# Residual rows moved to VectorE in a two-layer decoder trunk, with two smaller moves in the tail and the gate

## The chip, the cores and the metric

The kernel runs on one core of one Trainium2 chip. The metric is the device time of one execution in microseconds (us), the median of several runs. A run with a profile also gives its span, from the first to the last instruction, and for every instruction its engine, start and duration. The engines are named as in the profile: PE (TensorE, with PEld for its weight loads), DVE (VectorE), ACT (ScalarE), POOL (GpSimd) and SP (SyncE, here only a queue for DMAs).

## What is computed

Four sublayers follow one another on x of 512 rows (tokens) by 1024 columns: 0 is a hybrid mixer (sparse attention and a spatial gate), 1 and 3 are SwiGLU feed-forward layers (FFN) with 2816 hidden units, 2 is a gated short convolution (the "odd" layer). Each is wrapped in the same way:

```python
def residual_update(x, c, ada_w, ada_b, ln_g, ln_b, sublayer):
    shift, scale, gate = ada_modulation(c, ada_w, ada_b)     # silu(c) @ w + b, three rows of 1024
    out = sublayer(x * (1 + scale) + shift)
    return layer_norm(ALPHA * x + (1 + gate) * out, ln_g, ln_b)
```

All is float32; ALPHA is the square root of 2.

## The kernel before

**Tiles.** Rows are cut into four row tiles of 128 (`ST`), kept in one SBUF tensor `xr` of 128 x 4 x 1024. Weights come in units of 128 x 2048, loaded in two halves into `raw` (four buffers, SP's queue, L443). Every float32 operand of a matmul is split into a rounded high part and a remainder, so each product takes three matmuls: for a weight unit ACT makes `hi` (L472) and DVE makes `lo` (L476); weights of an output projection are first multiplied by the gate row, `raw` by `gateb` on DVE (L462). The class `Stream` does this some units ahead of PE, in the order in which they will be used.

**Stages.** An input tile (`in_tile`, matmuls on L524) is 24 matmuls of 128 x 512 into one of four PSUM buffers; ACT or DVE take it out, and `split` makes the high part (L1880, ACT) and the remainder (L1881, DVE) of the activation. An output chunk (`out_chunk`, matmuls on L536) adds eight output tiles of 128 x 512 into `xr` by DVE (`out_evac`, L541). The order on each engine's queue is the order in which the Python code issues the instructions; only sublayer 0 and the begin of sublayer 1 follow an order written out by hand.

**From one sublayer to the next.** `tail_norm` runs the last output chunk row tile by row tile. Per row tile: evacuation, statistics (`stats`, L569, L574), a Newton iteration for the inverse square root (`newton`, L635 to L646, nine instructions on 128 x 1), the normalisation of `xr` in place (`norm`, L611, DVE), PE transposes (L658), the affine of the next sublayer's modulation (ACT, L668), high part (ACT, L675) and remainder (`low`, L678, DVE) of the transposed tile `h`. While row tile 2 is handled, ACT has begun a weight unit of the next sublayer; its two remainders (L476) are issued when row tile 3 is. `start_in` then begins four input tiles on the first half of the rows (256 columns), so that the transposes of row tile 3, hooked in after the second of them, have time; the second halves follow.

**The residual.** After the normalisation `xr` holds the plain normalised value; what the next output chunks add to is ALPHA times LayerNorm's result. `Norm.rows` loads the rows of ln_g and ln_b to all partitions (POOL's DMA queue, L559, L560), and POOL scales them by -ALPHA and ALPHA (L562, L564); `Norm.residual` multiplies and adds them to `xr`, two POOL instructions of 128 x 1024 for each row tile (L628, L629). All four row tiles are issued right behind `start_in`, before the second halves.

**The modulation's gate.** `ada_steps` is a generator that is advanced by `background()`, once after each tile: it loads 512 KB of ada_w at a time into `ar` (two buffers, ACT's queue, L344), adds eight products to `acc` on DVE (L330, L332), and sums over partitions by a matmul against ones (L364), from which DVE makes half of the row `gateb` (L365). The last of these, the gate of sublayer 3, is appended at the start of the odd layer.

Of the kernel before, what the change touches and what calls it, by code (L numbers as in the profile page):

```python
# [11 lines left out]
ALU = mybir.AluOpType  # L12
# [6 lines left out]
ST = S // P  # L19
KT = D // P  # L20
HID = 2816
ALPHA = 4.0 ** 0.25
# [200 lines left out]
def trunk(ctx: ExitStack, tc: tile.TileContext, x, c, ada_w, ada_b, ln_g, ln_b, even_w_in,  # L223
# [320 lines left out]
    class Norm:  # L544
# [9 lines left out]
        def rows(self):  # L554
            s = self.s
            l, w = divmod(s, 2)
            self.rowg = fpool[0].tile([P, D], F32, name="rowg", tag="rowg", bufs=1)
            self.rowb = fpool[0].tile([P, D], F32, name="rowb", tag="rowb", bufs=1)
            pool.dma_start(self.rowg, ln_g[l, w:w + 1, :].to_broadcast([P, D]))  # L559
            pool.dma_start(self.rowb, ln_b[l, w:w + 1, :].to_broadcast([P, D]))  # L560
            a = 1.0 if s == 3 else ALPHA
            pool.tensor_scalar(self.rowg, self.rowg, -a, None, op0=ALU.mult)  # L562
            if s != 3:
                pool.tensor_scalar(self.rowb, self.rowb, a, None, op0=ALU.mult)  # L564

        def stats(self, t, half, c=slice(0, 512)):
            if half == 0:
# [7 lines left out]
            return mv  # L575

        def rstd(self, t):
            return self.newton(self.aggr(t), pool if self.s < 3 else dve if t == 3 else nc.scalar)

        def store(self, t, mv, y):  # L580

# [41 lines left out]
                f()  # L623
            self.lows = []

        def residual(self, t):
            z = xr[:, t, :]
            pool.tensor_tensor(z, z, self.rowg, op=ALU.mult)  # L628
            pool.tensor_tensor(z, z, self.rowb, op=ALU.add)  # L629

    def newton(e, var, v, hv, y, q):

# [1171 lines left out]
    def tail_norm(acts, us, norm):  # L1804

        ws.get(us[-1], 0)
        pend, conv = None, ()
        for t in range(ST):
            pp = [out_tile(half) for half in range(2)]
            if t == 0:  # L1810
                for half in range(2):
                    out_mms(pp[half], acts, us, t, half, range(3), True, False)
            for half in range(2):
                if t == 0:
                    out_mms(pp[half], acts, us, t, half, [3], False, True)
                    out_evac(pp[half], t, half)
                    norm.stats(t, half)
                else:
                    n = 256 if (norm.s, t, half) == (3, 3, 1) else 512
                    for a in range(0, 512, n):  # L1820
                        c = slice(a, a + n)
                        if a:
                            pp[half] = ps.tile([P, 512], F32, name="po", tag="tr")
                        out_mms(pp[half], acts, us, t, half, range(4), True, True, c)
                        out_evac(pp[half], t, half, c)
                        norm.stats(t, half, c)
                if norm.s < 3 and half == 0 and t:
                    norm.norm(t - 1, *pend)
                    norm.low()
            pend = norm.rstd(t)  # L1830
            if norm.s == 3:
                norm.store(t, *pend)
            if t == 2 and ws.ready < min(us[-1] + 3, len(ws.units)):
                conv = ws.pieces()
                for i in range(2):
                    if conv[0]:
                        conv[0](i, dve)
                    conv[1](i)
            if t == 3 and conv:
                for i in range(2):  # L1840
                    conv[2](i, dve)
            if t and norm.s != 3:
                norm.transpose(t - 1)
        if norm.s == 3:
            return
        norm.norm(3, *pend)
        norm.low()

    def start_in(units, norm):
# [29 lines left out]
    def split(f, a, k):  # L1879
        act(a[0][:, k, :], f, AF.Copy)  # L1880
        dve.tensor_tensor(a[1][:, k, :], f, a[0][:, k, :], op=ALU.subtract)  # L1881
# [12 lines left out]
    def run_ffn(s, prev, cfg):  # L1894
        sizes, starts, ins, outs = cfg
        norm = Norm(s)
        acts = {}
        for ci in range(6):
            acts[ci] = new_act()
            for pr in range(sizes[ci] // 2):  # L1900
                m = starts[ci] + 2 * pr
                ug, uu = ins[m]
                if m == 0:
                    tl = prev.tiles or start_in([(ug, 0), (ug, 1), (uu, 0), (uu, 1)], prev)
                    if s == 1:
                        prev.rows()
                    for t in range(ST):
                        prev.residual(t)
                if ci == 3 and pr == 0:
                    norm.rows()  # L1910
                sg = []
                for q in range(4):
                    u = (ug, uu)[q // 2]
                    if m == 0:
                        p = tl[q]
                        in_tile(p, u, q % 2, prev.h, prev.second, 2 if q < 2 else 1)
                    else:
                        p = pm.tile([P, S], F32, name="pi", tag="mm")
                        in_tile(p, u, q % 2, prev.h, ahead=3)
                    if q < 2:  # L1920
                        f = fp.tile([P, S], F32, name="sg", tag="sg", bufs=3)
                        act(f, p, AF.Silu)  # L1922
                        sg.append(f)
                    else:
                        f = sg[q - 2]
                        dve.tensor_tensor(f, f, p, op=ALU.mult)  # L1926
                        split(f, acts[ci], 2 * pr + q - 2)
                    background()
                if pr == 0 and ci > 0:
                    out_chunk(acts.pop(ci - 1), outs[ci - 1], sizes[ci - 1])  # L1930
                    if s == 1 and ci == 1:
                        bg.extend([ada_steps(2, (0, 1, 2, 3)), ada_steps(2, (4, 5)),
                                   ada_steps(3, (0, 1, 2, 3))])
        if s == 1:
            drain_background()
            mod_finish(2)
            mod_finish(3)
        tail_norm(acts_of(acts[5]), outs[5], norm)
        tail_hooks(norm)
        return norm  # L1940

    def run_odd(s, prev):
        norm = Norm(s)
        acts = {}
        bg.append(ada_steps(3, (4, 5)))
        for pr in range(4):
            uc, uz, ub = o_in[pr]
            if pr == 2:
                norm.rows()
            if pr % 2 == 0:  # L1950
                acts[pr // 2] = new_act()
            if pr == 0:
                tl = start_in([(uc, 0), (uc, 1), (uz, 0), (uz, 1)], prev)
                for t in range(ST):
                    prev.residual(t)
            cz = []
            for q in range(6):
                u = (uc, uz, ub)[q // 2]
                j = 2 * pr + q % 2
                if pr == 0 and q < 4:  # L1960
                    p = tl[q]
                    in_tile(p, u, q % 2, prev.h, prev.second, 2 if q < 2 else 1)
                else:
                    p = pm.tile([P, S], F32, name="pi", tag="mm")
                    in_tile(p, u, q % 2, prev.h, ahead=3)
                if q < 2:
                    f = fp.tile([P, S + 2], F32, name="cz", tag="cz", bufs=2)
                    pool.memset(f[:, 0:2], 0.0)
                    act(f[:, 2:], p, AF.Copy)
                    cz.append(f)  # L1970
                elif q < 4:
                    f = cz[q - 2]
                    dve.tensor_tensor(f[:, 2:], f[:, 2:], p, op=ALU.mult)
                    y = fp.tile([P, S], F32, name="y", tag="sg", bufs=3)
                    dve.tensor_scalar(y, f[:, 2:], pc[:, j, 10:11], None, op0=ALU.mult)
                    dve.scalar_tensor_tensor(y, f[:, 1:S + 1], pc[:, j, 9:10], y,
                                             op0=ALU.mult, op1=ALU.add)
                    dve.scalar_tensor_tensor(y, f[:, 0:S], pc[:, j, 8:9], y,
                                             op0=ALU.mult, op1=ALU.add)
                    cz[q - 2] = y  # L1980
                else:
                    f = cz[q - 4]
                    dve.tensor_tensor(f, f, p, op=ALU.mult)
                    split(f, acts[pr // 2], j % 4)
                background()
                if pr == 2 and q == 3:
                    out_chunk(acts[0], o_out[0], 4)
        drain_background()
        tail_norm(acts_of(acts[1]), o_out[1], norm)
        tail_hooks(norm)  # L1990
        return norm
# [33 lines left out]
```

## Time and profile before

| what | value |
|---|---|
| median of 3 runs | 1273.43 us (1273.17 to 1279.45) |
| the profiled execution | 1270.58 us |
| its span | 1268.9 us |
| mean granted TensorE clock in it | 0.986 |
| busy share PE, DVE, ACT, POOL | 95%, 63%, 35%, 18% |

In the rows of a timeline the first number is the start in us from the span's begin, the second the duration, then engine, line, operation and out<-in; `x4` merges four instructions, and a bracket gives the idle time of the engine before it and what ended that. A row of a table of waits reads: who waited, for whom, us in total, times, longest. A row of stretches gives for each of PE, PEld, DVE, ACT and POOL the busy us and the number of instructions, then the granted clock of PE (1.00 is full), the busy share of the DMA engines and GB/s. A row of one line gives the shortest, the median and the longest duration in ns, then the first and last start.

### The profile page before, as it was taken

Reading aid. Unit: us, or ns where it says so; the run is one execution under the profiler, and the core shown is the slowest. Engines: PE = TensorE matmul, PEld = TensorE weight load, DVE = VectorE, ACT = ScalarE, POOL = GpSimd, SP = SyncE. Lnnn points to the kernel's source line nnn. Section 1 sums busy time; section 2 is a strip of 40 time slices with the busy share of each in tenths; the row PEclk is TensorE's granted clock in tenths of the full one; section 3 lists DMA queues with packets and bytes.
Section 4 is the critical chain, followed back from the end, with each engine's and each line's share of the span. In section 5 each row is a group of like instructions: output and inputs, shape, how many; then the busy total and the mean of one; then the engine's idle time right before and its main releaser. Section 6 shows DMA issues by size and latency. Waiting matters only on the chain.

```text
span 1268.9 us, 15462 instructions
## 1 busy us (share of the span) xinstructions
PE 1205.6 (95%) x5939; PEld 987.7 (78%) x5939; DVE 797.1 (63%) x1264; ACT 446.3 (35%) x776; POOL 231.4 (18%) x283
## 2 busy tenths in 40 slices
PE   5999999899989999999998799999899999999996
PEld 4777767678878888888887688887888888888885
DVE  5776567886766665657567875466874353535446
ACT  2472257985232122213125232124332121313224
POOL 3230013485810000000005420002800000000005
PEclk9899999999999999999999899999999999999998
DMA  9794651241366554547431463240253232323301
GB/s 298 209 282 129 210 181 50 62 139 43 105 195 195 169 167 162 172 147 222 144 100 50 144 222 100 67 131 3 100 166 100 67 128 72 108 92 100 100 1 67
DMA packets 121466, 164.74 MB, mean 130 GB/s; under 512 B 5861, under 2 KB 87085, under 8 KB 121392
## 3 DMA queue, kind: packets, MB, share of 16 engines
q1 hardware_dynamic: 105552, 132.33, 33.4%
q10 hardware_dynamic: 14208, 26.75, 6.4%
q0 software_dynamic: 1632, 4.67, 1.2%
q8 instruction: 46, 0.75, 0.2%
q14 instruction: 28, 0.23, 0.1%
HBM read 161.63 MB, written 2.10 MB: 129 GB/s over the span
## 4 chain that ended last, share of the span: by engine, by line
PE 82%; DVE 9%; DMA 3%; issue 2%; ACT 2%; POOL 2%; SPq 0%; DVEq 0%; ACTq 0%
PE pi L524 45%; PE po L536 23%; PE pi L1267 5%; DVE h L678 2%; DVE lo L476 1%; PE ph L1456 1%; PE po L1106 1%; PE ptp L1623 1%; DMA ar<-in_ada_w_dram 1%; DVE xr L611 1%; PE pi L859 1%; DVE xr L541 1%; DVE bst L569 1%; PE pc L1023 1%; PE pvo L1638 1%
## 5 line engine op out<-in xcount | busy, mean ns | idle before, releaser
L524 PE MATMUL pi<-h,hi 128*128 128x512 f32 (+1 forms) x2016 | 580.1, 373 | 2.2 <-DVE h L678 2.2
L524 PEld LDWEIGHTS pi<-h,hi 128*128 128x128 f32 x2016 | 367.8, 190 | 70.0 <-DVE h L678 2.6
L524 PE MATMUL pi<-h,lo 128*128 128x512 f32 (+1 forms) x1008 | 373.9, 371 | 0.0
L472 ACT ACTIVATE hi<-raw 128x1024 fp32r<-128x1024 f32 (+1 forms) x186 | 187.4, 1045 | 285.9 <-PE po L536 105.9
L476 DVE TENSOR_TENSOR lo<-raw,hi 128x1024 fp32r<-128x1024 f32 (+1 forms) x178 | 223.9, 1296 | 94.6 <-ACT hi L472 92.9
L524 PEld LDWEIGHTS pi<-h,lo 128*128 128x128 f32 x1008 | 190.8, 189 | 33.3
L541 DVE TENSOR_TENSOR xr<-xr,po 128x512 f32<-128x512 f32 x129 | 87.5, 681 | 130.2 <-PE po L536 130.0
L536 PE MATMUL po<-hi,ah 128*128 128x512 f32 (+1 forms) x420 | 165.9, 395 | 3.5 <-DVE xr L541 3.3
L536 PE MATMUL po<-hi,al 128*128 128x512 f32 (+1 forms) x420 | 165.1, 393 | 0.0
L536 PE MATMUL po<-lo,ah 128*128 128x512 f32 (+1 forms) x420 | 165.0, 393 | 0.0
L536 PEld LDWEIGHTS po<-hi,ah 128*128 128x128 f32 x420 | 79.4, 189 | 22.8 <-DVE xr L541 5.3
L536 PEld LDWEIGHTS po<-hi,al 128*128 128x128 f32 x420 | 79.4, 189 | 18.0
L536 PEld LDWEIGHTS po<-lo,ah 128*128 128x128 f32 x420 | 79.4, 189 | 17.7
L1880 ACT ACTIVATE ah<-sg 128x512 fp32r<-128x512 f32 x44 | 27.8, 632 | 173.6 <-DVE sg L1926 173.6
L1926 DVE TENSOR_TENSOR sg<-sg,pi 128x512 f32<-128x512 f32 x44 | 30.2, 687 | 90.4 <-PE pi L524 83.7
L635 POOL TENSOR_SCALAR v<-mv 128x1 f32<-128x1 f32 x12 | 4.7, 394 | 406.6 <-DVE mv L574 406.4
L462 DVE TENSOR_TENSOR raw<-raw,gateb 128x1024 f32<-128x1024 f32 x60 | 75.3, 1292 | 4.3 <-DMA raw<-in_even_w_out_dram 4.2
L332 DVE SCALAR_TENSOR_TENSOR acc<-ar,cs,acc 128x512 f32<-128x512 f32 x84 | 64.9, 773 | 7.3 <-DMA ar<-in_ada_w_dram 5.5
L1922 ACT ACTIVATE sg<-pi 128x512 f32<-128x512 f32 x44 | 26.3, 598 | 120.9 <-PE pi L524 120.8
L588 POOL TENSOR_TENSOR xr<-xr,rowg 128x512 f32<-128x512 f32 x6 | 8.2, 1359 | 325.7 <-ACT xr L587 325.7
L1267 PE MATMUL pi<-hi,h 128*128 128x512 f32 (+1 forms) x192 | 59.8, 377 | 0.0
L1881 DVE TENSOR_TENSOR al<-sg,ah 128x512 fp32r<-128x512 f32 x44 | 33.1, 752 | 30.8 <-ACT ah L1880 30.8
(256 smaller groups left out, 1363.0 us busy)
## 6 DMA issues: line engine op xcount, KB each, us to landing
raw<-in_ffn_w_in_dram SPq DMA_DIRECT2D x88, 512.0 KB, 4.5
ar<-in_ada_w_dram ACTq DMA_DIRECT2D x48, 512.0 KB, 4.3
raw<-in_ffn_w_out_dram SPq DMA_DIRECT2D x44, 512.0 KB, 4.1
ar<-in_ada_w_dram SPq DMA_DIRECT2D x24, 512.0 KB, 5.3
raw<-in_odd_w_in_dram SPq DMA_DIRECT2D x24, 512.0 KB, 4.5
raw<-in_even_w_in_dram SPq DMA_DIRECT2D x10, 512.0 KB, 5.3
aw<-in_ada_w_dram SPq DMA_DIRECT2D x8, 512.0 KB, 6.3
aw<-in_ada_w_dram SPq DMA_DIRECT2D x4, 1024.0 KB, 8.9
```

The lines of the kernel that those rows point to most:

```text
L332: dve.scalar_tensor_tensor(acc, r, cs[:, k:k + 1], acc, op0=ALU.mult, op1=ALU.add)
L462: e.tensor_tensor(z[:, k, :], z[:, k, :], gateb[fold == 2], op=ALU.mult)
L472: act(hl[0][:, i * n0:i * n0 + n0], raw(i), AF.Copy)
L476: e.tensor_tensor(hl[1][:, sl], self.raw.pop(2 * u + i), hl[0][:, sl], op=ALU.subtract)
L524: mm(p[:, sl], w, h[z][k // 4][:, k % 4, sl], start=k == 0 and i == 0, stop=k == KT - 1 and i == 2)
L536: mm(p[:, c], s_, w[:, k % 2, c0], start=first and i == 0, stop=last and i == n - 1)
L541: dve.tensor_tensor(z, z, p[:, c], op=ALU.add)
L1267: mm(tiles[t], s_, w[:, q, :], start=k == 0 and z == 0, stop=k == 7 and z == 2)
L1880: act(a[0][:, k, :], f, AF.Copy)
L1881: dve.tensor_tensor(a[1][:, k, :], f, a[0][:, k, :], op=ALU.subtract)
L1922: act(f, p, AF.Silu)
L1926: dve.tensor_tensor(f, f, p, op=ALU.mult)
```

## The change

The residual is done by DVE with two `scalar_tensor_tensor` instructions to a row tile, which take ALPHA as their scalar, so that POOL no longer scales the rows (only sublayer 3's ln_g is still negated). They are issued one by one: in an FFN behind the tiles of the first two chunks, in the odd layer behind the last two tiles of the first pair and the six of the second. The Newton iteration of row tile 3 goes from POOL to DVE in sublayers 1 and 2 too. The normalisation of row tile 3 and the transposes of row tile 2 are issued ahead of the two weight remainders. The gate of sublayer 3 is appended at the odd layer's second pair, behind the six tiles of the first.

```diff
@@ Norm.rows
-            a = 1.0 if s == 3 else ALPHA
-            pool.tensor_scalar(self.rowg, self.rowg, -a, None, op0=ALU.mult)
-            if s != 3:
-                pool.tensor_scalar(self.rowb, self.rowb, a, None, op0=ALU.mult)
+            if s == 3:
+                pool.tensor_scalar(self.rowg, self.rowg, -1.0, None, op0=ALU.mult)
@@ Norm.rstd
-            return self.newton(self.aggr(t), pool if self.s < 3 else dve if t == 3 else nc.scalar)
+            return self.newton(self.aggr(t), dve if t == 3 else pool if self.s < 3 else nc.scalar)
@@ Norm.residual
-        def residual(self, t):
-            z = xr[:, t, :]
-            pool.tensor_tensor(z, z, self.rowg, op=ALU.mult)
-            pool.tensor_tensor(z, z, self.rowb, op=ALU.add)
+        def residual(self):
+
+            for t in range(ST):
+                z = xr[:, t, :]
+                dve.scalar_tensor_tensor(z, z, -ALPHA, self.rowg, op0=ALU.mult, op1=ALU.mult)
+                yield
+                dve.scalar_tensor_tensor(z, self.rowb, ALPHA, z, op0=ALU.mult, op1=ALU.add)
+                yield
@@ tail_norm
+            if t == 3 and norm.s != 3:
+                norm.norm(3, *pend)
+            if t and norm.s != 3:
+                norm.transpose(t - 1)
             if t == 3 and conv:
                 for i in range(2):
                     conv[2](i, dve)
-            if t and norm.s != 3:
-                norm.transpose(t - 1)
-        if norm.s == 3:
-            return
-        norm.norm(3, *pend)
         norm.low()
@@ run_ffn
-                    for t in range(ST):
-                        prev.residual(t)
+                    res = prev.residual()
...
+                    if ci < 2 and pr == 0:
+                        for _ in range((0, 1, 1, 1, 2, 1, 1, 1)[4 * ci + q]):
+                            next(res)
                     background()
@@ run_odd
-        bg.append(ada_steps(3, (4, 5)))
...
-                for t in range(ST):
-                    prev.residual(t)
+                res = prev.residual()
+            if pr == 1:
+                bg.append(ada_steps(3, (4, 5)))
...
+                if 4 <= 6 * pr + q < 12:
+                    next(res)
                 background()
```

## The prediction

> **What bounds the kernel now.** I read the page first, then the PE engine's own table of waits, then the timeline of each engine around those waits.
>
> ```profile
> span 1268.9 us, 15462 instructions
> ...
> PE 1205.6 (95%) x5939; PEld 987.7 (78%) x5939; DVE 797.1 (63%) x1264; ACT 446.3 (35%) x776; POOL 231.4 (18%) x283
> ```
>
> PE is the bound: only 63 us of the span are without a matmul. An edit that gives PE no less work can win only from these gaps and from the speed at which PE restarts after them. So the question is which gaps belong to the lines of the diff. The PE rows of the table of waits (total, times, longest):
>
> ```profile
> PE pt L658 <- DVE xr L611: 9.2, 4, 3.9
> ...
> PE pa L364 <- DVE acc L332: 8.2, 1, 8.2
> ...
> PE po L536 <- DVE xr L541: 4.0, 3, 3.3
> PE pi L524 <- DVE h L678: 2.2, 2, 1.1
> ```
>
> These four hang on the code around the change. In the PE timeline they stand at three places: the first FFN, the entry to the odd layer and the entry to the second FFN.
>
> ```profile
> 357.87 0.50 PE L536 MATMUL po<-hi,ah 128*128 128x512 f32 x1 [3.29 <-DVE xr L541]
> ...
> 688.98 0.28 PE L524 MATMUL pi<-h,lo 128*128 128x256 f32 x1
> 693.19 0.61 PE L658 MATMUL pt<-ident,xr 128*128 128x128 f32 x2 [3.93 <-DVE xr L611]
> ...
> 704.28 0.38 PE L524 MATMUL pi<-h,hi 128*128 128x256 f32 x1 [1.11 <-DVE h L678]
> ...
> 722.65 2.08 PE L364 MATMUL pa<-acc,ones 128*128 128x512 f32 x2 [8.21 <-DVE acc L332]
> ...
> 894.59 1.90 PE L658 MATMUL pt<-ident,xr 128*128 128x128 f32 x8 [3.93 <-DVE xr L611]
> ...
> 905.67 0.39 PE L524 MATMUL pi<-h,hi 128*128 128x256 f32 x1 [1.11 <-DVE h L678]
> ```
>
> Together 3.29 + 3.93 + 1.11 + 8.21 + 3.93 + 1.11 = 21.6 us. All end on DVE. Why DVE is late shows in five DVE rows, two POOL rows, and the minimum/median/maximum of two DVE lines over the whole run:
>
> ```profile
> 684.92 0.21 DVE L574 BATCH_NORM_AGGREGATE mv<-bst 128x2 f32<-128x12 f32 x1
> 685.05 2.31 DVE L476 TENSOR_TENSOR lo<-raw,hi 128x1024 fp32r<-128x1024 f32 x2
> 690.23 2.81 DVE L611 TENSOR_SCALAR xr<-xr,mv,y 128x1024 f32<-128x1024 f32 x1 [2.88 <-POOL y L646]
> 692.96 11.26 DVE L678 TENSOR_TENSOR h<-v,h 128x512 fp32r<-128x512 f32 x4
> ...
> 721.06 1.54 DVE L332 SCALAR_TENSOR_TENSOR acc<-ar,cs,acc 128x512 f32<-128x512 f32 x2 [4.02 <-DMA ar<-in_ada_w_dram]
> ```
>
> ```profile
> 690.15 2.34 POOL L628 TENSOR_TENSOR xr<-xr,rowg 128x1024 f32<-128x1024 f32 x1
> ...
> 709.07 2.74 POOL L629 TENSOR_TENSOR xr<-xr,rowb 128x1024 f32<-128x1024 f32 x1
> ```
>
> ```profile
> L611 DVE TENSOR_SCALAR xr<-xr,mv,y x12: 796/813/2812, 280.4 to 891.6; 128x1024 f32<-128x1024 f32 x12
> ```
>
> ```profile
> L678 DVE TENSOR_TENSOR h<-v,h x22: 673/693/2900, 297.1 to 902.7; 128x512 fp32r<-128x512 f32 x22
> ```
>
> From 690.15 to 711.8 POOL runs the eight residual instructions (L628, L629) back to back, and every DVE instruction in that stretch takes about as long as one POOL instruction: L611 2.81 us for 0.81, each L678 2.8 for 0.69. So three things are added up: the Newton iteration of the last tile on POOL lets DVE idle 2.88 us; then the normalisation is stretched by 2.0 us; then the four L678 by 8.4. The same pattern stands at 891.6. The gate's wait (L364) is the tail of it: its additions (L330, L332) queue behind the stretched DVE, hold the two ar buffers, and the next load is issued late (4.02 us of waiting for DMA).
>
> **The price of a gap isn't only the gap.** The granted clock (the number after the five engines' pairs) falls when PE restarts:
>
> ```profile
> 358.00:370.00 12.00, 12.00 (x45) 9.56 (x46) 8.90 (x11) 2.40 (x3) 0.00 (x0) 0.86 0.44 136
> ...
> 694.00:705.00 11.00, 9.89 (x73) 9.68 (x72) 11.00 (x5) 6.17 (x12) 10.84 (x5) 0.88 0.16 49
> 723.00:745.00 22.00, 22.00 (x85) 16.97 (x85) 19.86 (x25) 7.29 (x9) 7.20 (x6) 0.90 0.71 222
> ...
> 895.00:906.00 11.00, 9.89 (x70) 9.68 (x70) 11.00 (x5) 6.18 (x12) 10.84 (x5) 0.86 0.00 0
> ```
>
> Length times what is missing to 1.00: 12 x 0.14 = 1.7 us after the gap at 357.9; 11 x 0.12 = 1.3 after that at 693.2; 22 x 0.10 = 2.2 after that at 722.7; 11 x 0.14 = 1.5 after that at 894.6. Sum 6.7 us. [...]
>
> **The change, part by part.**
>
> *Residual off POOL.* 24 POOL instructions and the row scalings (L562, L564) go but for the last layer's; 24 DVE instructions of 128x1024 come. DVE has no two-input scalar instruction of that width in the trace. Rows near it:
>
> ```profile
> L332 DVE SCALAR_TENSOR_TENSOR acc<-ar,cs,acc x84: 735/751/2760, 376.1 to 737.8; 128x512 f32<-128x512 f32 x84
> ```
>
> ```profile
> L476 DVE TENSOR_TENSOR lo<-raw,hi x12: 1211/1222/1226, 743.9 to 784.5; 128x1024 fp32r<-128x1024 f32 x12
> ```
>
> At least 1.22 us (a plain two-input instruction of that width), at most 2 x 0.75 = 1.50 us (two of half width). I take 1.29, nearer the first, since of two halves one start-up falls away. 24 x 1.29 = 31 us on DVE (29 to 36), eight to a layer, at most two to a PE tile. They wait only for the two row loads, which now land as before; what queues behind them on DVE is the next evacuation or split.
>
> *First FFN.* The late evacuation at 357.87 came down this chain:
>
> ```profile
> 330.86 6.75 DVE lo L476 x2
> 337.61 6.68 DVE raw L462 x2
> 344.29 2.36 DVE lo L476 x2
> 346.67 6.21 DMA raw<-in_ffn_w_in_dram
> ```
>
> The first two rows are 4.4 and 4.3 us longer than the undisturbed 2.36 of the third. They release raw buffers, so the load of 6.21 us began 8.7 us late. Against that stand the six residual instructions that now precede it, 6 x 1.29 = 7.7 us; but three of them fall where DVE stood idle waiting for PE before 330. Following DVE's program order from 315 on without stretching and with the residuals in it, I get the raw load landing near 346 rather than 352.9, the last split at 352.3, the eighth residual until 353.4 and the first evacuation at 354.0; PE needs its bank at 354.58 (357.87 - 3.29). So the wait goes, with half a microsecond of margin, and perhaps 0.3 us stays at a later bank. Gain 3.3 + 1.7 - 0.3 = 4.7.
>
> *Newton of the last tile on DVE, normalisation ahead of the weight remainders.* The last layer already does this on DVE:
>
> ```profile
> 1258.11 0.24 DVE L574 BATCH_NORM_AGGREGATE mv<-bst 128x2 f32<-128x18 f32 x1
> ...
> 1260.39 1.06 DVE L593 SCALAR_TENSOR_TENSOR xr<-xr,mv,rowg 128x512 f32<-128x512 f32 x1
> ```
>
> 2.28 us from aggregate to its user. At the odd layer's entry the aggregate starts at 684.92, so L611 starts at 687.2 and ends at 688.0 instead of 693.0. PE ends its two half tiles at 689.26 and finds it ready. What is late next: the two L476 (2.31 us) now run 688.0 to 690.3, and the tile after the transposes needs them at about 690.1 to 690.4: I charge 0.2. Then L678 of tile 2 until 691.5, of tile 3 at about 695.9 (ACT's affine and copy below, twice in a row from 691, and one L678); PE comes to the second slices at 696 and needs the later half 1.4 us on.
>
> ```profile
> 695.90 1.51 ACT L668 ACTIVATE v<-pt,b,g 128x128 f32<-128x128 f32 x4 [8.50 <-DVE h L678]
> 697.44 0.63 ACT L675 ACTIVATE h<-v 128x512 fp32r<-128x512 f32 x1
> ```
>
> So 3.93 + 1.11 - 0.2 = 4.8 us at each of the two entries, and their clock, 1.3 and 1.5: 12.5.
>
> *Gate six tiles later.* Its eight ar loads leave ACT's queue at the entry and its 16 additions fall on full tiles, one load and 1.53 us of DVE to a tile of 5.48. Here residuals 3 to 8, the gate and the odd layer's own work meet. DVE in six tiles there, and the length of eight tiles:
>
> ```profile
> 748.00:781.00 33.00, 33.00 (x146) 27.12 (x145) 20.83 (x23) 8.60 (x10) 0.20 (x2) 1.00 0.45 140
> ```
>
> ```profile
> 814.64 43.85 PE pi L524 x192
> ```
>
> 20.8 + 6 x 1.53 + 6 x 1.29 = 37.7 us in 33: DVE falls 4.7 us behind (6 at 1.50 each). Four PSUM buffers let PE run three tiles ahead, 3 x 5.48 = 16.4 us, so PE doesn't feel it; the output chunk that follows has room. The gate's matmul comes two to three tiles after its last addition. Gain 8.2 + 2.2 = 10.4.
>
> **Sum:** 4.7 + 12.5 + 10.4 = 27.6 us. The profiled execution took 1270.6 (span 1268.9 and 1.7 around it): 1243.0. The median of the runs, 1273.4, lies 2.9 higher; the forecast on that footing is 1273.4 - 27.6 = **1246**.
>
> **Rivals.** (1) *The next wait at the entries.* If the transposes or the tile behind them find DVE late by the moved L476 (2.31 us) and this still costs the clock (1.4), some 3.7 us stay at each: 1253. For it: L476 ends within 0.3 us of PE's need; against: 2.31 us is below any gap that shows a clock loss. (2) *The gate's wait only moves*: loads, additions and residuals collide in the second pair of the odd layer, and PE stops at L364 for the same 10.4: 1256. For it: DVE is over 100% there; against: its loads are a tile apart. (3) *The stretching isn't from the residuals*: then L678 and L476 stay long and only the Newton step (2.9 us twice) and the gate are won, some 16 us, less what the new work costs on a DVE that stays slow: 1257 to 1270. Against: L678 is 0.69 everywhere else. (4) *Slower: DVE becomes the bound* where the residuals sit. If none of the new work is hidden it costs 24 x 1.29 to 1.50 = 31 to 36 us against 27.6: 1277 to 1282. It decides from a backlog over 16.4 us in the odd layer, or over four output tiles in the FFNs; I find 4.7 to 6. [...]
>
> **Numbers.** Forecast 0.69 (own range 1241 to 1250), rival 1 0.11, rival 2 0.10, rival 3 0.06, rival 4 0.04. The low end is the full 21.6 + 6.7 = 28.3 us taken from the profiled execution's 1270.6, less 2 for what I didn't count; the high end takes in rivals 1 and 2. Range 1239 to 1258. About 0.5% (6.4 us) is what a measurement here can tell from no change: forecast, rivals 1 and 2 and half of 3 are faster by more, 0.93; the other half of 3 and some of 4 the same, 0.04; slower 0.03.
>
> **What would show it.** Right: L678 and L611 with maxima near 0.7 and 0.8; no PE wait over 1 us on L658, L364, L524 between 300 and 930; the new DVE instructions at 1.2 to 1.5 us; granted clock 1.00 at both entries. Wrong: PE waiting for L476 behind the transposes, for L364 in the odd layer's third pair, or for evacuations at the first output chunk of an FFN.

## The result, and the profile after

The changed kernel takes 1243.0 us (median of 4 runs, 1241.4 to 1244.2) against 1273.5 (median of 4): a ratio of 0.9765, 95% interval 0.9748 to 0.9782, so 30 us less. The forecast was 1246, 27.6 less. The profiled execution has a span of 1239.5 us and a mean granted clock of 0.995 (0.986 before).

First, where the time went. In the chain that ended last (rows of start, length, engine, tile and line) the first FFN begins with the same 60 matmuls in both kernels, and the tail of each of the sublayers 1, 2 and 3 with the same 21, which gives four marks. Before:

```profile
303.26 7.18 PE pi L524 x60
...
657.12 4.89 PE po L536 x21
...
858.50 4.89 PE po L536 x21
...
1234.44 4.90 PE po L536 x21
```

After:

```profile
303.73 7.17 PE pi L524 x60
...
652.41 4.89 PE po L536 x21
...
836.23 4.89 PE po L536 x21
...
1205.20 4.90 PE po L536 x21
```

| stretch | before | after | won | forecast |
|---|---|---|---|---|
| to the begin of the first FFN (sublayer 0) | 303.3 | 303.7 | -0.5 | 0 |
| from there to the tail of sublayer 1 (first FFN) | 353.9 | 348.7 | 5.2 | 4.7 |
| from there to the tail of 2 (odd layer's entry and the gate) | 201.4 | 183.8 | 17.6 | 16.5 |
| from there to the tail of 3 (second FFN's entry) | 375.9 | 369.0 | 7.0 | 6.3 |
| from there to the end | 34.5 | 34.3 | 0.2 | 0 |

In PE's table of waits of the changed kernel only these two rows on lines of the three sublayers are left. The line numbers behind the edit have moved by two, L609 is the normalisation that was L611 and L680 the remainder of h that was L678:

```profile
PE pt L660 <- DVE xr L609: 1.4, 2, 0.7
...
PE po L536 <- DVE xr L541: 0.7, 2, 0.3
```

The two of the first row are the short ones before the transposes of the first row tile, which were there before too; those of the second row lie in sublayer 0 (at 290.0 and 299.5). DVE at the odd layer's entry, and in a second fence PE's stretches at both entries:

```profile
680.18 0.21 DVE L572 BATCH_NORM_AGGREGATE mv<-bst 128x2 f32<-128x12 f32 x1
...
682.48 0.81 DVE L609 TENSOR_SCALAR xr<-xr,mv,y 128x1024 f32<-128x1024 f32 x1
683.20 2.35 DVE L476 TENSOR_TENSOR lo<-raw,hi 128x1024 fp32r<-128x1024 f32 x2
685.47 1.29 DVE L680 TENSOR_TENSOR h<-v,h 128x512 fp32r<-128x512 f32 x2
688.46 0.69 DVE L680 TENSOR_TENSOR h<-v,h 128x512 fp32r<-128x512 f32 x1 [1.70 <-ACT h L677]
690.51 0.69 DVE L680 TENSOR_TENSOR h<-v,h 128x512 fp32r<-128x512 f32 x1 [1.36 <-ACT h L677]
```

```profile
678.00:690.00 12.00, 12.00 (x104) 12.00 (x103) 9.10 (x20) 7.85 (x20) 0.00 (x0) 1.00 0.27 89
...
862.00:874.00 12.00, 12.00 (x105) 12.00 (x103) 8.94 (x20) 8.00 (x20) 0.00 (x0) 1.00 0.28 89
```

From aggregate to normalisation 2.30 us (forecast 2.28), every instruction at its undisturbed length, PE busy for all of both stretches at full clock. The new instructions and the gate's additions, as lines:

```profile
L628 DVE SCALAR_TENSOR_TENSOR xr<-xr,rowg x12: 1215/1218/1221, 317.5 to 904.8; 128x1024 f32<-128x1024 f32 x12
```

```profile
L332 DVE SCALAR_TENSOR_TENSOR acc<-ar,cs,acc x84: 743/752/755, 372.5 to 769.3; 128x512 f32<-128x512 f32 x84
```

1.22 us each (the second instruction, L630, likewise), the lower of the two bounds; and L332, whose longest was 2760 ns, is 755 at most.

### The profile page after: what moved, and what is told of

Read it like the earlier page. It is cut to its first block, busy times and chain, and to the rows that moved or that the text cites. A ratio compares the mean times of both kernels' runs of the same rounds, so it can differ in the third digit from the quotient of the medians.

```text
span 1239.5 us, 15445 instructions
## 1 busy us (share of the span) xinstructions
PE 1197.7 (97%) x5939; PEld 981.9 (79%) x5939; DVE 781.1 (63%) x1306; ACT 445.3 (36%) x776; POOL 137.4 (11%) x235
## 4 chain that ended last, share of the span: by engine, by line
PE 91%; DVE 3%; DMA 2%; ACT 2%; issue 1%; POOL 0%; SPq 0%; ACTq 0%; DVEq 0%
PE pi L524 51%; PE po L536 25%; PE pi L1269 5%; PE pi L861 1%; PE ph L1458 1%; DMA ar<-in_ada_w_dram 1%; PE po L1108 1%; PE ptp L1625 1%; PE pt L660 1%; PE pc L1025 1%; PE pi L864 1%; PE pvo L1639 1%; PE pvo L1640 1%; DMA ad<-in_ada_w_dram 0%; DMA aw<-in_ada_w_dram 0%
## 5 line engine op out<-in xcount | busy, mean ns | idle before, releaser
L476 DVE TENSOR_TENSOR lo<-raw,hi 128x1024 fp32r<-128x1024 f32 (+1 forms) x178 | 211.0, 1225 | 84.3 <-ACT hi L472 82.7
L536 PE MATMUL po<-hi,ah 128*128 128x512 f32 (+1 forms) x420 | 165.8, 395 | 0.2
L536 PE MATMUL po<-hi,al 128*128 128x512 f32 (+1 forms) x420 | 164.5, 392 | 0.0
L536 PE MATMUL po<-lo,ah 128*128 128x512 f32 (+1 forms) x420 | 164.3, 391 | 0.0
L536 PEld LDWEIGHTS po<-hi,ah 128*128 128x128 f32 x420 | 79.0, 188 | 19.9 <-DVE xr L541 1.9
L536 PEld LDWEIGHTS po<-lo,ah 128*128 128x128 f32 x420 | 79.1, 188 | 17.7 <-issue 0.2
L536 PEld LDWEIGHTS po<-hi,al 128*128 128x128 f32 x420 | 79.0, 188 | 17.8
L462 DVE TENSOR_TENSOR raw<-raw,gateb 128x1024 f32<-128x1024 f32 x60 | 70.9, 1219 | 4.1 <-DMA raw<-in_even_w_out_dram 4.1
L332 DVE SCALAR_TENSOR_TENSOR acc<-ar,cs,acc 128x512 f32<-128x512 f32 x84 | 63.0, 750 | 3.3 <-DMA ar<-in_ada_w_dram 1.5
L1882 DVE TENSOR_TENSOR al<-sg,ah 128x512 fp32r<-128x512 f32 x44 | 30.5, 693 | 30.7 <-ACT ah L1881 30.7
L670 ACT ACTIVATE v<-pt,b,g 128x128 f32<-128x128 f32 x88 | 32.9, 454 | 44.0 <-PE pt L660 35.7
```

The lines of the kernel that those rows point to most:

```text
L332: dve.scalar_tensor_tensor(acc, r, cs[:, k:k + 1], acc, op0=ALU.mult, op1=ALU.add)
L462: e.tensor_tensor(z[:, k, :], z[:, k, :], gateb[fold == 2], op=ALU.mult)
L476: e.tensor_tensor(hl[1][:, sl], self.raw.pop(2 * u + i), hl[0][:, sl], op=ALU.subtract)
L536: mm(p[:, c], s_, w[:, k % 2, c0], start=first and i == 0, stop=last and i == n - 1)
L670: act(v[:, q, :], p[:, q, :], AF.Identity, scale=g1[s][:, k:k + 1], bias=b1[s][:, k:k + 1])
```

## The experiments

All times are medians; ratios are against the kernel before on the same chip (median 1272.5 for the first four rows, 1272.9 for the next four, 1273.2 for the last), with 95% intervals.

| kernel | us | ratio |
|---|---|---|
| residual on DVE alone | 1250.8 | 0.982 (0.979 to 0.984) |
| gate later alone | 1261.3 | 0.991 (0.989 to 0.993) |
| Newton and order of the tail alone | 1276.8 | 1.004 (1.002 to 1.006) |
| all but the gate | 1245.0 | 0.978 (0.976 to 0.981) |
| all, residual in one block | 1242.3 | 0.975 (0.973 to 0.977) |
| all, with eight POOL instructions of two inputs at each entry | 1255.2 | 0.987 (0.983 to 0.991) |
| all, with eight POOL memsets | 1243.2 (2 runs) | 0.976 (0.972 to 0.979) |
| all, with eight POOL instructions of one input | 1248.7 (2 runs) | 0.980 (0.977 to 0.984) |
| all, every Newton iteration of sublayers 1 and 2 on DVE | 1242.6 | 0.976 (0.974 to 0.977) |

**The residual alone.** The kernel before with the hunks of `rows`, `residual` and its issue in `run_ffn` and `run_odd`, and no other:

```diff
-            pool.tensor_tensor(z, z, self.rowg, op=ALU.mult)
-            pool.tensor_tensor(z, z, self.rowb, op=ALU.add)
...
+                dve.scalar_tensor_tensor(z, z, -ALPHA, self.rowg, op0=ALU.mult, op1=ALU.mult)
+                yield
+                dve.scalar_tensor_tensor(z, self.rowb, ALPHA, z, op0=ALU.mult, op1=ALU.add)
+                yield
```

> The kernel before with the residual on DVE alone; Newton of the last row tile on POOL, the order of the tail and the early gate stay. Theory (POOL's residual stretches DVE, and the gate's wait is the tail of that): L678 and L611 at 0.7 and 0.8 us; the wait before the last transposes shrinks from 3.93 to about 1.9 us (the Newton part stays) and costs no clock; the waits on L678 and at 357.9 go; the wait at L364 shrinks from 8.2 to under 1 us though the gate isn't moved. 1273.4 - (4.7 + 2 x (2.0 + 1.1 + 1.4) + 10) = about 1250 us. Rival (the three edits each win their own stall, as the sum was laid out): L364 keeps its 8.2 us and the lost clock, about 1259 us.

Measured 1250.8 us. The longest L680 takes 721 ns and the longest L609 814. Of PE's waits on these lines one row is left, but for a single 0.3 us on L536, and none at L364:

```profile
PE pt L660 <- DVE xr L609: 5.2, 4, 1.9
```

So the gate's wait of 8.2 us goes without touching the gate: it was the tail of POOL's stretch, as the theory has it, and the rival's 1259 falls. One thing in the expectation was wrong, that the 1.93 us gap left at each entry costs no clock. PE's stretches behind the first of them (686.90 to 688.83):

```profile
688.00:690.00 2.00, 1.17 (x6) 1.20 (x7) 1.88 (x3) 0.05 (x1) 0.00 (x0) 0.70 0.86 282
690.00:692.00 2.00, 2.00 (x11) 2.00 (x10) 0.00 (x0) 1.97 (x5) 0.00 (x0) 0.50 0.03 11
692.00:694.00 2.00, 2.00 (x18) 2.00 (x17) 0.69 (x1) 1.97 (x6) 0.00 (x0) 0.95 0.00 0
```

2 x (0.30 + 0.50 + 0.05) = 1.7 us lost (a little of it while PE still waited), as much as the kernel before loses behind its gap of 3.93 (4 us at 0.56 and 0.58).

**The gate alone.** The kernel before, with its line moved:

```diff
-        bg.append(ada_steps(3, (4, 5)))
...
+            if pr == 1:
+                bg.append(ada_steps(3, (4, 5)))
```

> The kernel before with only the gate begun six tiles later; residual on POOL. Theory: the wait at L364 goes, since the loads and additions now run after POOL's stretch; the waits at the transposes, on L678 and at 357.9 stay: 1273.4 - 10.4 = about 1263 us. Rival (the wait only moves): 1270 to 1274 us with a wait at L364 in the third pair.

Measured 1261.3. L364 no longer stands among PE's waits, the others stand as before:

```profile
PE pt L658 <- DVE xr L611: 9.1, 4, 3.9
PE po L536 <- DVE xr L541: 4.2, 3, 3.6
...
PE pi L524 <- DVE h L678: 2.2, 2, 1.1
```

The move alone wins 11.2 us against POOL's stretch, and 10.5 by the chain's marks (from the tail of sublayer 1 to that of sublayer 2 201.4 us before, 190.9 here): the 10.4 of the forecast's term, on the kernel it was read from.

**Newton and the order of the tail alone.**

```diff
-            return self.newton(self.aggr(t), pool if self.s < 3 else dve if t == 3 else nc.scalar)
+            return self.newton(self.aggr(t), dve if t == 3 else pool if self.s < 3 else nc.scalar)
...
+            if t == 3 and norm.s != 3:
+                norm.norm(3, *pend)
+            if t and norm.s != 3:
+                norm.transpose(t - 1)
             if t == 3 and conv:
...
```

> The kernel before with only Newton of the last row tile on DVE and the normalisation ahead of the weight remainders; residual on POOL. Theory: POOL's Newton was what held the residual back until 690; without it POOL begins the residual some 8 us earlier, right after the third tile's Newton, and stretches DVE there: the wait before the last transposes stays or grows to about 4 to 6 us, L678 of the second tile too is near 2.8 us, time 1272 to 1282 us. Rival (the Newton step is worth its idle time): 2 x 2.9 us and some clock won, 1264 to 1268 us.

Measured 1276.8 (ten runs), a little slower than before. POOL and DVE at the odd layer's entry:

```profile
681.93 2.36 POOL L628 TENSOR_TENSOR xr<-xr,rowg 128x1024 f32<-128x1024 f32 x1
```

```profile
682.01 2.83 DVE L611 TENSOR_SCALAR xr<-xr,mv,y 128x1024 f32<-128x1024 f32 x1 [0.46 <-POOL y L646]
684.76 5.63 DVE L678 TENSOR_TENSOR h<-v,h 128x512 fp32r<-128x512 f32 x2
690.31 0.67 DVE L541 TENSOR_TENSOR xr<-xr,po 128x512 f32<-128x512 f32 x1
...
695.44 6.71 DVE L476 TENSOR_TENSOR lo<-raw,hi 128x1024 fp32r<-128x1024 f32 x2
```

The residual now begins at 681.93 instead of 690.15, since the last Newton no longer stands before it on POOL's queue, and stretches the third tile's normalisation and the remainders instead. PE waits in more places, each shorter:

```profile
PE pi L524 <- DVE lo L476: 6.3, 4, 1.6
PE pt L658 <- DVE xr L611: 5.6, 4, 2.1
PE pi L524 <- DVE h L678: 4.5, 6, 1.5
PE po L536 <- DVE xr L541: 4.0, 3, 3.3
PE pa L364 <- DVE acc L332: 1.9, 1, 1.9
```

The wait of 4 to 6 us that the expectation put before the last transposes isn't there, the longest on L658 is 2.1; the time came out as expected. By the chain's marks the odd layer's stretch is 3.2 us shorter than in the kernel before (198.2 against 201.4), since the wait at L364 falls from 8.2 to 1.9, and the second FFN's, which has no such wait to lose, is 5.5 us longer (381.4 against 375.9). An edit that is worth 5.8 us on top of the residual's (below) is worth nothing, and rather a loss, without it.

**All but the gate.** The changed kernel, with `bg.append(ada_steps(3, (4, 5)))` back at the start of `run_odd`.

> The changed kernel with the gate begun at the start of the odd layer again. Theory (the gate's wait was the tail of the stretch): 1243 to 1246 us, a wait of 0 to 2 us at L364 and ACT held now and then by the ar buffers. Rival (the move itself is worth 10.4 us): 1253 us with a wait of about 8 us at L364.

Measured 1245.0. One wait comes back:

```profile
PE pa L364 <- DVE acc L332: 1.7, 1, 1.7
```

So the move of the gate is worth some 2.0 us once POOL is out of the way, about the size of that wait. The single times of the two kernels overlap, but the chain's marks agree: the odd layer's stretch takes 185.8 us here and 183.8 in the changed kernel. The tail's two edits are worth 1250.8 - 1245.0 = 5.8: twice the 1.93 us gap and the 1.7 of clock are 7.3, less this 1.7 at L364, which the kernel with the slower entry doesn't have.

**The residual in one block.**

```diff
-                    res = prev.residual()
+                    for _ in prev.residual():
+                        pass
```

(the same in `run_odd`, and the two places with `next(res)` dropped)

> The changed kernel with a layer's eight residual instructions issued on DVE in one block, right behind the half tiles, instead of one or two to a PE tile. Theory: DVE stands idle there for about 6 us, waiting for PE, and a block of 8 x 1.14 = 9.1 us makes the next evacuations 3 us late, which the four PSUM buffers cover: 1242 to 1245 us, no new wait of PE. Rival (the spreading is what keeps PE fed): waits of PE at the first output chunk or the first pair, 3 us or more a layer, 1250 us and above.

Measured 1242.3, no new wait of PE. Spreading the eight instructions over PE tiles is not what wins; that they are on DVE is.

**Does POOL stretch DVE, or do both get in each other's way on `xr`?** Three kernels add POOL work to the changed kernel that isn't needed for anything, into a gate row that is not in use there (`z`), begun when the last row tile is normalised:

```diff
+            pool.tensor_copy(z[:, 0:1], xr[:, 3, 0:1])
+            for _ in range(8):
+                pool.tensor_tensor(z, self.rowg, self.rowb, op=ALU.mult)
```

> The changed kernel with eight extra POOL instructions of 128x1024 with two inputs at the two entries (odd layer, second FFN), on rows and a spare tensor that share no data with DVE's work there, begun when the last row tile is normalised. Theory (POOL's reading stretches DVE whatever it works on): h remainders and weight remainders at about 2.8 us for some 22 us, PE waits of 2 to 6 us at each entry, 1250 to 1260 us. Rival (the stretch came from both engines working on xr): durations as in the changed kernel, 1243 us.

Measured 1255.2. DVE and POOL at the odd layer's entry, and PE's wait that returned (L685 is the remainder of h here):

```profile
683.15 0.81 DVE L609 TENSOR_SCALAR xr<-xr,mv,y 128x1024 f32<-128x1024 f32 x1
683.88 2.35 DVE L476 TENSOR_TENSOR lo<-raw,hi 128x1024 fp32r<-128x1024 f32 x2
686.15 11.45 DVE L685 TENSOR_TENSOR h<-v,h 128x512 fp32r<-128x512 f32 x4
697.53 6.84 DVE L476 TENSOR_TENSOR lo<-raw,hi 128x1024 fp32r<-128x1024 f32 x2
```

```profile
685.23 24.03 POOL L636 TENSOR_TENSOR gateb<-rowg,rowb 128x1024 f32<-128x1024 f32 x8
```

```profile
PE pi L524 <- DVE h L685: 7.9, 4, 2.9
```

The four remainders take 11.45 us, as they did before the change (11.26), though these eight POOL instructions share no data with them. So what stretches DVE here is POOL's two-input work itself (24.03 us for the eight), not that both work on `xr`.

With memsets in place of the multiplication (`pool.memset(z, 0.0)`):

> As the kernel with eight extra POOL instructions, but memsets of 128x1024, which read nothing. Theory (it is POOL's reading that DVE's second input waits for): h remainders at 0.7 us, about 1243 us. Rival (any POOL instruction stretches DVE): remainders near one POOL instruction each, 1250 us.

Measured 1243.2. The eight memsets are shorter, about 1 us each, but all four remainders fall beside them (the last at 692.62), and each takes the time that it has without any POOL work there (0.69; the first two make 1.29 together, as in the changed kernel):

```profile
687.58 1.29 DVE L685 TENSOR_TENSOR h<-v,h 128x512 fp32r<-128x512 f32 x2
```

```profile
686.63 8.04 POOL L636 MEMSET gateb<- 128x1024 f32 x8
```

With one input (`pool.tensor_scalar(z, self.rowg, 2.0, None, op0=ALU.mult)`):

> As the kernel with eight extra POOL instructions, but of one input (row times 2.0). Theory: it reads, so DVE's two-input instructions are stretched to about one POOL instruction each, 2.5 to 3 us, and the time is near that of two inputs, 1250 to 1260 us. Rival (only POOL's two-input instructions do it): about 1243 us.

Measured 1248.7, between the two, but not for the expected reason. DVE and POOL:

```profile
686.54 2.13 DVE L685 TENSOR_TENSOR h<-v,h 128x512 fp32r<-128x512 f32 x2
690.36 0.69 DVE L685 TENSOR_TENSOR h<-v,h 128x512 fp32r<-128x512 f32 x1 [1.70 <-ACT h L682]
692.42 1.40 DVE L685 TENSOR_TENSOR h<-v,h 128x512 fp32r<-128x512 f32 x1 [1.36 <-ACT h L682]
...
710.22 0.75 DVE L1987 SCALAR_TENSOR_TENSOR y<-cz,pc,y 128x512 f32<-128x512 f32 x1 [7.24 <-POOL cz L1979]
```

```profile
685.62 24.52 POOL L636 TENSOR_SCALAR gateb<-rowg 128x1024 f32<-128x1024 f32 x8
```

Some DVE instructions are about 0.5 to 0.85 us longer and others not at all; none takes as long as a whole POOL instruction, and PE has no gap over 0.7 us at either entry. What shows is another thing: a small memset for the convolution (L1979) stands behind the eight on POOL's queue, DVE waits 7.24 us for it, and PE later has one gap of 2.94 us, with some 1.7 us of clock lost behind it (0.50 and 0.67 over 4 us). The entry to the second FFN separates the two: the same eight stand there with the same DVE durations (2.13, 0.69, 1.40) and no convolution behind them, and by the chain's marks its stretch takes 369.8 us against 369.0 in the changed kernel and 376.3 in the one with two inputs. So the stretch by one-input instructions costs 0.9 us there, and most of this kernel's 5.7 us is the queue. The theory that any reading POOL instruction does the same as one with two inputs falls; so the memset kernel's theory has its 0.69 us and 1243, but its reason, that DVE's second input waits for POOL's reading, is not shown.

**Every Newton iteration on DVE**, to see whether the last two short waits can be had:

```diff
-            return self.newton(self.aggr(t), dve if t == 3 else pool if self.s < 3 else nc.scalar)
+            return self.newton(self.aggr(t), dve if t == 3 or self.s < 3 else nc.scalar)
```

> The changed kernel with the Newton iteration of all row tiles of sublayers 1 and 2 on DVE. The only waits of PE on DVE left at the entries are 0.66 and 0.68 us before the transposes of the first row tile, where L609 waits for POOL's Newton. Theory: DVE has 2 us of idle time behind each tile's statistics, so both waits go and nothing else moves: 1.3 us, 1241 to 1242.5 us. Rival (the nine small instructions delay the evacuations of the next tile, whose banks PE waits for): 1243 to 1246 us.

Measured 1242.6, not to be told from 1243.0. The wait only shrinks:

```profile
PE pt L660 <- DVE xr L609: 1.1, 2, 0.5
```

The normalisation is issued behind the next tile's first evacuation and its statistics, and these are what it waits for once the Newton iteration is early.

## Why the prediction was right, and where not

**What bounds the kernel, and why DVE was late: right.** Of the 21.6 us of gaps all but the two of 1.93 went with the residual alone: 17.7 us, and with them 4.1 us of lost clock (7.5 before, by the working below, and 2 x 1.7 left); the measured 21.7 of 30 us is their sum to 0.1. So these were the stretching by POOL's residual; the 3.9 that stayed were the Newton iteration on POOL, as the prediction had it. The kernel with foreign POOL work shows the stretching by itself.

**The sum: right within 2.9 us.** The steps came out at 5.2, 17.6 and 7.0 us against 4.7, 16.5 and 6.3, all three on the low side. That the tail of sublayer 1 came just 4.7 us earlier is luck: 0.5 us went the other way in sublayer 0, before the change begins. The begin of the first FFN lies between 303.3 and 306.1 in the eleven traces, while the stretch behind it takes 353.9 to 354.1 us in the three with the residual on POOL and 348.7 in the eight others. The 0.3 us that were to stay there, and the 0.2 us charged at each entry for the weight remainders, weren't spent (PE is busy throughout the stretches shown). The term for the clock left out the microsecond from 693, at 0.63, the 0.4 us from 722.6, at 0.50, and the stretch 890 to 895, at 0.96: with them it is 1.7 + 1.7 + 2.4 + 1.7 = 7.5 us, not 6.7. Of the 30.5 us 29.4 show between the two traces; the rest lies between the profiled executions and the medians. The low end works out at 1270.6 - 28.3 - 2 = 1240.3, where the ranges say 1239 and 1241; nothing hung on it. The price of the new instruction was 1.22 us, not 1.29; it was the lower bound, that of a plain two-input instruction, and nothing hung on it. The start-up that was to fall away was the author's estimate; the trace before shows 1.22 us for a full width (L476) against 2 x 0.69 for two halves (L678).

**The odd layer's crowded pair: right.** DVE was to fall 4.7 us behind there. PE's input tiles run without a break up to the gate's matmul, in the chain that ended last:

```profile
685.40 71.92 PE pi L524 x384
757.32 0.86 PE pa L364 x2
```

Tiles of 5.48 us counted back from 757.32 put the ends of the second pair's last two tiles at 740.9 and 746.4. DVE takes them up here:

```profile
745.79 0.68 DVE L1986 TENSOR_TENSOR y<-y,pi 128x512 f32<-128x512 f32 x1
...
750.37 0.68 DVE L1986 TENSOR_TENSOR y<-y,pi 128x512 f32<-128x512 f32 x1
```

4.9 and 4.0 us late, inside the 16.4 that the PSUM buffers cover; so the rival in which DVE becomes the bound fell.

**What each edit is worth: the sum's layout misleads.** It books 10.4 us to the gate's move and 12.5 to the entries, as though they were separate. Alone, the residual wins 21.7, the gate 11.2, the tail loses 4.3; that adds to 28.6, near the 30 measured, but by chance: on top of the others the gate is worth 2.0 and the tail, on top of the residual, 5.8. Added in that order, 21.7 + 5.8 + 2.0 = 29.5, they do make up the whole. The prediction called the gate's wait the tail of the stretch and should have drawn the consequence, that the first edit removes most of it. For the forecast of the whole it made no difference, since each gap was counted once.

**The clock: the term was right but for its size, a remark on it wrong.** That 2.31 us is "below any gap that shows a clock loss" was read from the gaps of one trace. The residual-only kernel lost 1.7 us behind a gap of 1.93, as much as the kernel before behind its gap of 3.29 (12 us at 0.86).

Rival 1 (weight remainders late) and rival 2 (the gate's wait only moves) fell with the two rows of waits that are left; rival 3 (the stretching is not from POOL's residual) with the undisturbed L609, L680 and L332.

## What to carry to other kernels

Before giving elementwise work to POOL because it is idle, look at what DVE does in the same stretch: two POOL instructions to a row tile cost PE 22 us here, though POOL was busy 18% and DVE had room for the work. Look at the minimum, median and maximum of a DVE line; where the maximum is near a POOL instruction's length (here L678's 2.90 us and L628's 2.34 to 3.38), look at that POOL instruction first; here 17.7 of PE's 21.6 us of gaps went with it. And edits that each cure a symptom of one cause are not additive: one of them alone even cost time here (the tail's, 4.3 us), by starting the cause earlier.

## What the runs showed of the hardware

- While POOL ran instructions of two SBUF inputs (the residual, 2.3 to 3.4 us each; the foreign ones, 24.03 us for eight), a DVE instruction with two SBUF inputs took about as long as one of them: L678 2.8 us for 0.69, and L685 11.45 us for four. Beside POOL memsets L685 kept its 0.69. Beside POOL instructions of one input (24.52 us for eight) it took 0.69 or 1.4; why so much less stays open.
- Some DVE instructions with one SBUF tensor as input were stretched beside POOL's residual too: L611 took 2.81 us for 0.81 at 690.23 and L330 2.60 for 0.48 at 704.14 in the kernel before. In the kernel with the tail's edits alone L611 took 1.46 at 694.05, and the statistics (L569, 128x512) kept their 0.69 at 691.02.
- A DVE evacuation with one operand in PSUM kept its length in the middle of POOL's residual: 0.67 us at 690.31 in the kernel with the tail's edits alone, where POOL's L629 ran from 689.92 to 692.62.
- In these runs the length of a gap of PE alone didn't settle whether the clock fell behind it. Behind 1.93 us it fell to 0.50 (above). In the kernel with POOL instructions of two inputs PE stood still for 2.88 and then 1.15 us at the odd layer's entry (691.94 to 694.82 and 696.51 to 697.66), and the stretches there are at 1.00; at the second FFN's entry it stood still for 2.74 and 1.10 us (880.33 to 883.07 and 884.76 to 885.86), and the clock was at 0.50 from 885 to 891, some 3 us lost:

```profile
694.00:696.00 2.00, 1.18 (x10) 1.18 (x11) 2.00 (x2) 2.00 (x3) 1.92 (x2) 1.00 0.00 0
696.00:698.00 2.00, 0.85 (x8) 0.65 (x6) 2.00 (x2) 0.11 (x1) 1.92 (x2) 1.00 0.00 0
...
885.00:887.00 2.00, 1.14 (x5) 1.14 (x6) 2.00 (x2) 0.00 (x0) 1.92 (x2) 0.50 0.00 0
887.00:889.00 2.00, 2.00 (x11) 2.00 (x11) 2.00 (x1) 0.39 (x1) 1.92 (x2) 0.50 0.00 0
```

What decides it stays open.
